# A hybrid decoder block on one core: five operations reordered around the second feed-forward head

## The chip, the cores and the metric

The kernel runs on one core of one Trainium2 chip. The metric is the device time of one execution in microseconds (us), the median of several runs. The profile shows one further execution of the same kernel; its engines are TensorE (PE, with its weight loads as PEld), VectorE (DVE), ScalarE (ACT), GpSimd (POOL) and SyncE (SP, which issues loads).

## The reference

One decoder layer on 512 tokens of width 1024, in float32. A conditioning vector c gives nine vectors: a shift, a scale and a gate for each of three sub-layers.

```python
mod = silu(c) @ w_ada + b_ada                        # nine vectors: sh1 sc1 gt1 sh2 sc2 gt2 sh3 sc3 gt3
u = modulate(rmsnorm(h, g_norm_ffn1), sh1, sc1)
h = h + 0.5 * gt1 * swiglu(u, w_ffn1_in, w_ffn1_out)
u = modulate(rmsnorm(h, g_norm_mix), sh2, sc2)
h = h + gt2 * token_mixing(u, ...)                   # pooling branch and dilated attention, gated, then @ w_out
u = modulate(rmsnorm(h, g_norm_ffn2), sh3, sc3)
h = h + 0.5 * gt3 * swiglu(u, w_ffn2_in, w_ffn2_out)
return rmsnorm(h, g_final)

def rmsnorm(x, g):       return x * rsqrt(mean(x * x, -1) + EPS) * g
def modulate(x, sh, sc): return x * (1 + sc) + sh
def swiglu(u, w_in, w_out):
    a, b = split(u @ w_in, 2)                        # 2816 columns each
    return (silu(a) * b) @ w_out
```

The change lies where token mixing ends and the second swiglu begins: the last output blocks of `merged @ w_out`, the norm of the result, and the first products of `u @ w_ffn2_in`.

## The kernel before, in words

**Layout.** Activations lie feature-major: H[k] is block k (128 features) of the residual stream, with 512 tokens, in two token halves A (0 to 255) and B (256 to 511). A float32 product is made of three matmuls on values split in two: every operand x has a high part (a rounded copy, made by ACT) and a low part (x minus the high part, made by DVE), and `mm3` adds hi·uh, hi·ul and lo·uh. So u, the normed input, exists as UH and UL.

**Weights.** They arrive as chunks of 128x1024 by loads on SP's queue, in a planned order. `split_hi` (ACT, L377, tile whi) and `split_lo` (DVE, L389, tile wlo) turn the next chunk into its two parts in a ring; `split(n)` does both up to chunk n; `look(ahead)` fetches and splits up to `ahead` chunks beyond the current one; `fetch` issues loads into free buffers. Some chunks of the second feed-forward net are sums of others, made by DVE (L312) or by an accumulating copy that POOL issues (L320): its products use a fast matrix multiplication of Strassen's kind, with seven products on 2x2 blocks instead of eight.

**`out_tail`** makes the last output blocks m = 5, 6, 7 of the mixing layer: first half A of each, then half B of each. Per block and half, `tail_step` adds the gated bank to H (DVE, L600) and ACT squares the result (L601); DVE adds the square to the sum of squares (L651, tile AR). The lambdas in `put` are these adds, and `do` runs them. In the middle of the matmuls of block 6, half B, `stats_t` sums half A over partitions by matmuls with ones (L512), takes the root on ACT (L514) and the reciprocal on DVE (L517). Ahead of block 7, half B, `spread` transposes the result over all partitions (L522), and `norm_steps` begins: for each block a norm on DVE (L535), UH on ACT (L547) and UL on DVE (L565).

**`head`** follows: four weight tiles (the first two pairs of columns) times u. Half A goes in twelve steps, the last four of which take blocks 4 to 7 with all four tiles; half B goes in eight steps. The norms of half B are made during half A. After step 8 of half A and steps 2 and 5 of half B a further chunk is split, as far as the ring has room.

**Rows of u.** The first of the block products need u also as a plain float32 array; for half B and for blocks 4 to 7 of half A, ACT writes these rows (L552, tile X). Rows of half B are written at once; those of half A wait in the list `rows`.

**`ffn2`** calls the head, then makes the sums of blocks of u for the fast multiplication: `u_steps` returns four sums (x22, x21, x11, x12) and the pairs of high and low parts (s0 to s3, ACT L757 and DVE L758, tiles SH and SL) made from them. The first seven products (`duo`, with `product`, L794 to L796) take u itself, then the parts of s0 (B), s1 (A), and so on.

**Order.** Every engine runs its instructions in the order in which the program issues them. The order of each queue is written out by hand, and the change edits this order.

Of the kernel before, what the change touches and what calls it, by code (L numbers as in the profile page):

```python
# [11 lines left out]
AF = mybir.ActivationFunctionType  # L12
# [153 lines left out]
class Kernel:  # L166
# [430 lines left out]
    def tail_step(self, m, hs, bank, gate, s):  # L597

        Hm = self.H[m][:, hs]
        self.nc.vector.scalar_tensor_tensor(Hm, bank[:, hs], gate[:, m:m + 1], Hm, op0=OP.mult, op1=OP.add)  # L600
        self.nc.scalar.activation(s, Hm, AF.Square)  # L601

    def out_tail(self, ms, ksrc, gate, nxt, squares, beside=None):


        nc = self.nc
        tiles, starts, put, rest = {}, {}, [], self.spare()
        A, Bh = slice(0, HT), slice(HT, T)
        step = None
        self.held = self.pos  # L610
        for h, hs in enumerate((A, Bh)):
            for m in ms:
                bank = self.nb()
                if h == 0:
                    starts[m] = self.pos
                    tiles[m] = ksrc(m)
                    starts[m + 1] = self.pos
                if h == 0 and m == ms[0]:
                    nc.scalar.preload_act_table(AF.Sqrt)
                behind = h == 1 and m == ms[1]  # L620
                if self.done < self.pos + 4 and not behind:
                    self.split_hi()
                ks = tiles[m]
                if h == 0 and m == ms[0]:
                    self.settle(bank, ks[0][0], ks[0][2])
                for i, (hi, lo, uh, ul) in enumerate(ks):
                    if behind and i == len(ks) // 2:
                        self.stats_t(rest[0], A)
                        if self.done < self.pos + 4:
                            self.split_hi()  # L630
                        if self.half and len(self.half[1]) > 1:
                            self.split_lo(True)
                    if h == 1 and m == ms[2] and i == 0:
                        self.spread(rest[0], A)
                        step = self.norm_steps(nxt, A)
                        if nxt == 2:
                            step.three()
                        step(0)
                        self.split_lo()
                        self.fetch()  # L640
                    self.mm3(bank[:, hs], hi, lo, uh[:, hs], ul[:, hs], i == 0, i == len(ks) - 1)
                if step and m == ms[-1]:
                    step.low()
                    step.high()
                s = squares(m)[:, :HT]
                self.tail_step(m, hs, bank, gate, s)
                if h == 1:
                    self.held = starts[m + 1]
                    if step:
                        step(1 if m != ms[-1] else 3)  # L650
                put.append(lambda s=s, hs=hs: nc.vector.tensor_tensor(self.acc[:, hs], self.acc[:, hs], s, op=OP.add))  # L651
                do = lambda: [put.pop(0)() for _ in range(len(put))]
                if nxt == 2 and h == 0 and m == ms[-1]:
                    do()
                if not behind:
                    self.split_lo()
                    self.fetch()
                if beside and h == 0 and m == ms[0]:
                    beside()
                if h == 0 or m != ms[1]:  # L660
                    do()
        self.stepA = step

    def head(self, n, banks, table, between=(), beside={}):

        nc = self.nc
        A, Bh = slice(0, HT), slice(HT, T)
        self.held = self.pos
        stepA, stepB = self.stepA, self.norm_steps(n, Bh)
        w = [self.take() for _ in banks]  # L670

        both, late = list(range(4)), (0, 1, 2)
        steps = [(k, late) for k in range(4)] + [(k, (3,)) for k in range(4)] + [(k, both) for k in range(4, KT)]
        for h, hs in enumerate((A, Bh)):
            for i, (k, which) in enumerate(steps if h == 0 else [(k, both) for k in range(KT)]):
                if h == 0:
                    if i == 4:
                        self.stats_t(self.spare()[1], Bh)
                        nc.scalar.preload_act_table(table)
                    stepA(min(i, 5) + 2)  # L680
                    if i == 8:
                        self.spread(self.spare()[1], Bh)
                    if i > 7:
                        stepB(i - 8)
                        if n == 2 and i == 8:
                            stepB.low()
                            while self.rows:
                                self.rows.pop(0)()
                else:
                    stepB(k + 3)  # L690
                for f in beside.get((h, i), ()):
                    f()
                for j in which:
                    self.mm3(banks[j][:, hs], *w[j][k], self.UH[k][:, hs], self.UL[k][:, hs], k == 0, k == KT - 1)
                if (h, i) in ((0, 8), (1, 2), (1, 5)):
                    if h and between:
                        between.pop(0)()
                    if n == 2 and (h, i) == (1, 2):
                        stepB.high()
                        stepB.low()  # L700
                    self.split(self.done)
                    self.fetch()
        for f in between:
            f()
        self.held = None
# [68 lines left out]
    def step(self):  # L774

        self.now += 1
        due = [f for t, f in self.put if t <= self.now]
        self.put = [x for x in self.put if x[0] > self.now]
        for f in due:
            f()  # L780
# [421 lines left out]
    def ffn2(self):  # L1202
        self.put, self.now = [], 0
        self.negate(2)
        bk = [self.nb() for _ in range(4)]
        (a11, a12), (a21, a22) = self.U4
        (x22, x21, x11, x12), (s2, s1, s0, s3) = self.u_steps(2)
        self.ready = True
        self.rows.pop(0)()
        self.head(2, bk, AF.Silu, beside={(0, 6): self.whole(a11, 0)})  # L1210
        for f in (x22, s0[0], x21):
            f()
        h0, h1 = (self.ffn_silu(j, bk[2 * j]) for j in range(2))
        for f in (x11, s1[0], s0[1], s1[1]):
            f()
        late = self.block_hidden(0)
        two = lambda: self.look(2)
        b4, b5 = (self.banks[(self.bi + i) % 6] for i in range(2))

        def begin():  # L1220
            two()
            x12()
            s2[0]()
            self.free += self.rawx[1:]

        def posts():
            two()
            self.ffn_post(0, h0, bk[1])
            self.ffn_post(1, h1, bk[3])

        def more():
            self.free += self.rawx[:1]

        def end():
            self.open_first()
            self.banks, self.bi = [bk[1], bk[2], b4, b5, bk[0], bk[3]], 0

        self.ffn(2, 2, ((begin,), (posts, s2[1]), (two, *s3, more), (self.look,), (*late[:4], self.look),
                        (late[4], late[6], self.look, late[5], late[7]), (self.look, end)))

# [1057 lines left out]
```

## Time and profile before

| what | value |
|---|---|
| median of 3 runs | 958.99 us |
| the 3 runs | 957.89, 958.99, 968.86 us |
| the profiled execution, its own time | 969.29 us |
| its span in the profile | 967.5 us |
| mean granted clock of TensorE | 0.999 |
| PE busy | 959.3 us, 99% of the span |
| DVE busy | 842.2 us, 87% |
| ACT busy | 545.4 us, 56% |
| POOL busy | 90.5 us, 9% |

A row of a timeline gives start, length, engine, line, operation, written tile, read tiles, shape and count, and in brackets the idle time of the engine ahead of it with what ended it. A row of the waits gives the waiter, what it waited for, the sum in us, how often, and the longest. A row of the window table gives the window, its length, then busy time and number of instructions for PE, PEld, DVE, ACT and POOL, the granted clock, the share of the DMA engines and their GB/s. Lengths of neighbouring instructions on one engine overlap a little, so the distance between starts tells what an instruction takes of a queue.

### The profile page before, as it was taken

To read this page: it belongs to the slowest core of one execution; us is meant where nothing else is said; L and a number is where in the kernel's file an instruction comes from. 1 tells how busy PE (TensorE), PEld (TensorE's weight loads), DVE (VectorE), ACT (ScalarE), POOL (GpSimd) and SP (SyncE) were. 2 spreads that over 40 slices of the span, in tenths; PEclk is the share of its full clock that TensorE was granted. 3 is DMA by queue.
4 is the path that set the end of the run, shared out by engine and by line. 5 is a ranking of instruction groups with operands and counts; after the bars stand their busy time and mean duration, and the time that the engine had idled before them with its cause. 6 is when DMAs were issued, how large, how long until landed. Compare 5 with 4: busy or idle time off the path is not lost.

```text
span 967.5 us, 18319 instructions
## 1 busy us (share of the span) xinstructions
PE 959.3 (99%) x7352; PEld 907.7 (94%) x7352; DVE 842.2 (87%) x1241; ACT 545.4 (56%) x829; POOL 90.5 (9%) x110
## 2 busy tenths in 40 slices
PE   9999999999999999999999999999999999999997
PEld 7888999999999999788899998999999999999997
DVE  7989999899998788886979768989998988879886
ACT  6453666665745453454565552477755656556555
POOL 0000100100010003007200000011011001000002
PEclk9999999999999999999999999999999999999999
DMA  9856776776868548857365446646766566665632
GB/s 357 283 191 240 209 218 166 207 207 152 223 170 246 174 153 254 260 189 197 77 186 158 137 144 224 206 102 185 200 166 161 140 173 164 166 153 140 163 81 88
DMA packets 55304, 176.81 MB, mean 183 GB/s; under 512 B 7857, under 2 KB 11569, under 8 KB 54962
## 3 DMA queue, kind: packets, MB, share of 16 engines
q1 hardware_dynamic: 44800, 141.82, 44.6%
q0 software_dynamic: 9840, 33.30, 19.2%
q8 instruction: 57, 0.93, 0.4%
q10 hardware_dynamic: 578, 0.53, 0.2%
q14 instruction: 29, 0.24, 0.1%
HBM read 135.36 MB, written 2.24 MB: 142 GB/s over the span
## 4 chain that ended last, share of the span: by engine, by line
PE 90%; DVE 4%; DMA 2%; ACT 1%; issue 1%; POOL 0%; SPq 0%; POOLq 0%; DVEq 0%; ACTq 0%
PE bank L795 15%; PE bank L794 15%; PE bank L796 15%; PE bank L424 6%; PE bank L425 6%; PE bank L426 6%; PE bank L1176 5%; PE bank L1175 5%; PE bank L1177 5%; PE bank L2219 2%; PE bank L2222 2%; PE bank L2224 1%; DVE wlo L389 1%; DMA v<-wada 1%; PE bank L1862 1%
## 5 line engine op out<-in xcount | busy, mean ns | idle before, releaser
L389 DVE TENSOR_TENSOR wlo<-raw,whi 128x1024 fp32r<-128x1024 f32 (+3 forms) x148 | 164.9, 1123 | 37.7 <-ACT whi L377 37.5
L794 PE MATMUL bank<-UH,whi 128*128 128x256 f32 x704 | 195.9, 278 | 0.0
L796 PE MATMUL bank<-UH,wlo 128*128 128x256 f32 x704 | 195.9, 278 | 0.0
L795 PE MATMUL bank<-UL,whi 128*128 128x256 f32 x704 | 195.9, 278 | 0.0
L389 DVE TENSOR_TENSOR wlo<-X,whi 128x1024 fp32r<-128x1024 f32 (+3 forms) x138 | 147.0, 1077 | 25.5 <-ACT whi L377 25.4
L377 ACT ACTIVATE whi<-raw 128x1024 fp32r<-128x1024 f32 (+3 forms) x148 | 141.3, 968 | 22.9 <-DMA raw<-wf1o 6.4
L377 ACT ACTIVATE whi<-X 128x1024 fp32r<-128x1024 f32 (+3 forms) x138 | 127.2, 942 | 42.9 <-DVE X L312 39.1
L794 PEld LDWEIGHTS bank<-UH,whi 128*128 128x128 f32 x704 | 133.5, 190 | 0.2
L795 PEld LDWEIGHTS bank<-UL,whi 128*128 128x128 f32 x704 | 132.2, 188 | 0.0
L796 PEld LDWEIGHTS bank<-UH,wlo 128*128 128x128 f32 x704 | 132.2, 188 | 0.0
L795 PE MATMUL bank<-SL,whi 128*128 128x256 f32 x432 | 120.5, 279 | 0.0
L796 PE MATMUL bank<-SH,wlo 128*128 128x256 f32 x432 | 120.4, 279 | 0.0
L794 PE MATMUL bank<-SH,whi 128*128 128x256 f32 x432 | 120.4, 279 | 0.0
L794 PEld LDWEIGHTS bank<-SH,whi 128*128 128x128 f32 x432 | 82.1, 190 | 0.0
L795 PEld LDWEIGHTS bank<-SL,whi 128*128 128x128 f32 x432 | 81.1, 188 | 0.2 <-DVE SL L758 0.2
L796 PEld LDWEIGHTS bank<-SH,wlo 128*128 128x128 f32 x432 | 81.1, 188 | 0.0
L424 PE MATMUL bank<-UH,whi 128*128 128x256 f32 (+1 forms) x240 | 80.4, 335 | 0.0
L425 PE MATMUL bank<-UL,whi 128*128 128x256 f32 (+1 forms) x240 | 79.2, 330 | 0.1
L426 PE MATMUL bank<-UH,wlo 128*128 128x256 f32 (+1 forms) x240 | 79.1, 330 | 0.0
L802 ACT ACTIVATE ev<-bank 128x512 f32<-128x512 f32 x54 | 32.1, 595 | 54.0 <-PE bank L796 53.8
L1175 PE MATMUL bank<-HI,whi 128*128 128x256 f32 x224 | 62.5, 279 | 0.0
L1176 PE MATMUL bank<-HK,whi 128*128 128x256 f32 x224 | 62.5, 279 | 0.0
(411 smaller groups left out, 2423.7 us busy)
## 6 DMA issues: line engine op xcount, KB each, us to landing
raw<-wmix SPq DMA_DIRECT2D x44, 512.0 KB, 4.2
raw<-wf1i SPq DMA_DIRECT2D x32, 512.0 KB, 5.7
raw<-wf2i SPq DMA_DIRECT2D x29, 512.0 KB, 4.5
ada<-wada SPq DMA_DIRECT2D x24, 512.0 KB, 6.0
X<-raw POOLq DMA_DIRECT2D x24, 512.0 KB, 5.2
xs<-wada SPq DMA_DIRECT2D x17, 512.0 KB, 6.0
X<-wf2i SPq DMA_DIRECT2D x15, 512.0 KB, 4.5
X<-wf1i SPq DMA_DIRECT2D x11, 512.0 KB, 4.3
```

The costliest lines, as they stand in the source:

```text
L377: self.nc.scalar.activation(self.hi[:, y], r[:, x], AF.Copy)
L389: self.nc.vector.tensor_tensor(self.lo[:, y], r[:, x], self.hi[:, y], op=OP.subtract)
L424: M(ps, hi, uh, start=start, stop=False)
L425: M(ps, hi, ul, start=False, stop=False)
L426: M(ps, lo, uh, start=False, stop=stop)
L794: M(o, hi, uh, start=start and p == 0 and k == 0, stop=False, skip_group_check=True)
L795: M(o, hi, ul, start=False, stop=False, skip_group_check=True)
L796: M(o, lo, uh, start=False, stop=k == 3, skip_group_check=True)
L802: copy = lambda o, x, f=1.0: nc.scalar.activation(o, x, AF.Copy, scale=f)
L1175: M(o, hi, uh, start=start and m % 2 == 0 and k == 0, stop=False, skip_group_check=True)
L1176: M(o, hi, ul, start=False, stop=False, skip_group_check=True)
L1177: M(o, lo, uh, start=False, stop=k == 1, skip_group_check=True)
```

## The change

Five edits of order, all in the second head; no instruction is added or removed.

1. *Root ahead of a square.* In `out_tail`, the square of block 5, half B, is held back until `stats_t` has issued the root of half A, and the add of that square runs behind the low part of a chunk, in the middle of block 6.
2. *u's rows behind a split.* In `head`, the deferred rows of u are written after the split and the fetch at step 8 of half A, not ahead of them.
3. At step 2 of half B, the high part of the next chunk is issued, then UL of block 7, then the chunk's low part; before, UL of block 7 came two steps later, behind the low part.
4. *First block sum's low part ahead of the third sum.* In `ffn2`, the low part of s0 is issued ahead of x11.
5. *A chunk ahead of the second.* The call that splits a chunk (`two`) is issued ahead of the high part of s1, not at the start of the first product.

```diff
     def tail_step(self, m, hs, bank, gate, s):
...
-        self.nc.scalar.activation(s, Hm, AF.Square)
+        return lambda: self.nc.scalar.activation(s, Hm, AF.Square)

     def out_tail(self, ms, ksrc, gate, nxt, squares, beside=None):
...
-        tiles, starts, put, rest = {}, {}, [], self.spare()
+        tiles, starts, put, squared, rest = {}, {}, [], [], self.spare()
+        do = lambda: [put.pop(0)() for _ in range(len(put))]
...
                         self.stats_t(rest[0], A)
+                        while squared:
+                            squared.pop(0)()
                         if self.done < self.pos + 4:
                             self.split_hi()
                         if self.half and len(self.half[1]) > 1:
                             self.split_lo(True)
+                        do()
...
-                self.tail_step(m, hs, bank, gate, s)
+                square = self.tail_step(m, hs, bank, gate, s)
+                first = nxt == 2 and h == 1 and m == ms[0]
+                if first:
+                    squared.append(square)
+                else:
+                    square()
...
-                if h == 0 or m != ms[1]:
+                if h == 0 or m != ms[1] and not first:
                     do()

     def head(self, n, banks, table, between=(), beside={}):
...
                         if n == 2 and i == 8:
                             stepB.low()
-                            while self.rows:
-                                self.rows.pop(0)()
...
                     if n == 2 and (h, i) == (1, 2):
                         stepB.high()
                         stepB.low()
-                    self.split(self.done)
+                        self.split_lo()
+                        self.split_hi()
+                        stepB(6)
+                        stepB.low()
+                    self.split(self.done - bool(self.half))
                     self.fetch()
+                    while self.rows:
+                        self.rows.pop(0)()

     def ffn2(self):
...
-        for f in (x11, s1[0], s0[1], s1[1]):
+        two = lambda: self.look(2)
+        for f in (s0[1], x11, two, s1[0], s1[1]):
             f()
         late = self.block_hidden(0)
-        two = lambda: self.look(2)
...
         def begin():
-            two()
             x12()
```

More of the change, by code (lines that the diff above doesn't have):

```diff
@@ L651, in out_tail @@
                 put.append(lambda s=s, hs=hs: nc.vector.tensor_tensor(self.acc[:, hs], self.acc[:, hs], s, op=OP.add))
-                do = lambda: [put.pop(0)() for _ in range(len(put))]
                 if nxt == 2 and h == 0 and m == ms[-1]:
```

## The prediction

> **What bounds the kernel now.** I read the page first, for the engine that carries the end, then one window table, then the waits of TensorE (PE) in the window of the change, then the timelines of PE, VectorE (DVE) and ScalarE (ACT) around each wait.
>
> ```profile
> span 967.5 us, 18319 instructions
> PE 90%; DVE 4%; DMA 2%; ACT 1%; issue 1%; POOL 0%; SPq 0%; POOLq 0%; DVEq 0%; ACTq 0%
> ...
> 612.00:656.00 44.00, 43.74 (x378) 43.13 (x377) 38.66 (x71) 30.28 (x55) 4.02 (x4) 1.00 0.46 122
> 656.00:949.00 293.00, 293.00 (x2493) 293.00 (x2492) 258.96 (x324) 179.51 (x245) 24.35 (x29) 1.00 0.61 154
> ```
>
> PE carries 90% of the chain that ended last. The window from 612 to 656 us holds everything the change touches; there PE is busy 43.74 of 44.00 us, and from 656 to 949 us all of 293.00 (the columns are PE, PEld, DVE, ACT, POOL). So the change can win only what PE waits in this window, and a DVE or ACT that gets ahead there wins nothing afterwards. DVE is busy 38.66 of the 44 us, so it is the engine that makes PE wait.
>
> A busy PE may hide a late start, since a matmul that waits on an operand is partly counted as busy. The waits of the same window give three with PE or its weight loads as the waiter, and the PE timeline gives their true size by the starts:
>
> ```profile
> PEld bank L425 <- DVE UL L565: 0.3, 1, 0.3
> PEld bank L522 <- DVE r L517: 0.3, 1, 0.3
> PEld bank L795 <- DVE SL L758: 0.2, 1, 0.2
> 623.08 0.28 PE L426 MATMUL bank<-v,wlo 128*128 128x256 f32 x1
> 623.48 0.43 PE L522 MATMUL bank<-cst,r 128*128 128x128 f32 x2
> 640.83 0.38 PE L424 MATMUL bank<-UH,whi 128*128 128x256 f32 x1
> 641.35 0.39 PE L425 MATMUL bank<-UL,whi 128*128 128x256 f32 x1
> 641.58 0.28 PE L426 MATMUL bank<-UH,wlo 128*128 128x256 f32 x1
> 652.35 0.28 PE L794 MATMUL bank<-SH,whi 128*128 128x256 f32 x1
> 652.62 0.39 PE L795 MATMUL bank<-SL,whi 128*128 128x256 f32 x1
> ```
>
> 128x256 matmuls normally start 0.115 us apart (18 of them from 626.61 to 628.65 in the next fence, 0.113 each; I use 0.115, since single gaps are 0.11 or 0.12). Against that: the transposes that spread the root (L522) start 0.40 after the matmul ahead of them, 0.29 too late. UL of the second half's third block is 0.52 behind its predecessor, 0.41 too late, and the matmul after it starts 0.23 later, another 0.12: a wait for an operand costs the wait and a restart of 0.12. The low part of the first block sum (SL) is 0.27 behind, 0.16 too late, and I count the same 0.12 behind it. Together 0.29 + 0.53 + 0.28 = **1.10 us**, the most that the change can take off by shortening waits: 0.11% of the span.
>
> **Part 1, the root ahead of a square.** Rows of DVE and ACT, then PE:
>
> ```profile
> 622.47 0.42 ACT L601 ACTIVATE gc<-H 128x256 f32<-128x256 f32 x1 [2.08 <-DVE H L600]
> 622.79 0.24 ACT L514 ACTIVATE r<-bank,eps 128x2 f32<-128x2 f32 x1
> 622.92 0.43 DVE L651 TENSOR_TENSOR AR<-AR,gc 128x256 f32<-128x256 f32 x1 [0.55 <-ACT gc L601]
> 622.93 1.14 ACT L377 ACTIVATE whi<-raw 128x512 fp32r<-128x512 f32 x2
> 623.26 0.16 DVE L517 RECIPROCAL r<-r 128x2 f32<-128x2 f32 x1
> 623.59 0.69 DVE L389 TENSOR_TENSOR wlo<-raw,whi 128x512 fp32r<-128x512 f32 x1 [0.17 <-ACT whi L377]
> 624.19 0.48 DVE L600 SCALAR_TENSOR_TENSOR H<-bank,mod,H 128x256 f32<-128x256 f32 x1
> 625.76 0.48 DVE L565 SCALAR_TENSOR_TENSOR UL<-ev,mod,UH 128x256 fp32r<-128x256 f32 x1
> 627.94 0.48 DVE L565 SCALAR_TENSOR_TENSOR UL<-ev,mod,UH 128x256 fp32r<-128x256 f32 x1
> 621.36 0.60 PE L512 MATMUL bank<-ones,AR 128*128 128x128 f32 x4
> 626.61 0.28 PE L425 MATMUL bank<-UL,whi 128*128 128x256 f32 x1
> 628.65 0.28 PE L425 MATMUL bank<-UL,whi 128*128 128x256 f32 x1
> ```
>
> The sums over partitions (L512) end at 621.36 + 0.60 = 621.96, but the root (L514) stands behind a square (L601) that waits for H until 622.47, and the reciprocal (L517) stands behind the add of that square. With the root first it can start near 622.1 (an estimate: 621.96 and a short way to ACT), end near 622.35, and the reciprocal ends by about 622.6, ahead of the 623.19 at which PE comes to the transposes. The wait of 0.29 goes.
>
> What is late next: the square still starts at 622.47, since H releases it; the copies of the next chunk (whi L377) follow at 622.79 instead of 622.93, 0.14 earlier; DVE's low part (L389) follows at 623.45 instead of 623.59. But the add, which ran from 622.92 in time that DVE had free, now stands behind this low part, in DVE's full stretch. It takes 623.26 - 622.92 = 0.34 of the queue. H of the next block (L600, 624.19) then starts 0.34 - 0.14 = 0.20 later, and so does all that is queued behind: three norms, UL of block 0 (625.76, L565), UL of block 2 (627.94). UL of block 0 would be done at 625.96 + 0.48 = 626.44 and usable about 0.06 later (UL at 640.81 + 0.48 against PE's 641.35, below), at 626.50. PE comes to it at 626.61 - 0.29 = 626.32: a new wait of 0.18 and a restart of 0.12. That is 0.30 given back for 0.29 won. UL of block 2 is usable at 628.14 + 0.54 = 628.68 against 628.65, so a second restart may come on top. **I take 0.0 for this part**; its bounds are -0.29 (DVE is not later, and the gain carries through) and +0.15 (the second restart as well).
>
> The Trainium skill (VectorE: DVE Perf Modes, "The DRAIN you can't avoid") says that the next DVE operation does not start until the pipe of the one before has emptied, and leaves operations that nothing holds to another section. By the plain rule the added step costs the add's whole 0.43 instead of 0.34, and this part would be +0.09 instead of 0.0. The rows 622.92 and 623.26 speak against it: the reciprocal starts 0.34 after the add.
>
> **Part 2, u's rows behind the split.** In step 8 of the head's first half, ACT writes row copies of u ahead of the split of the next chunk:
>
> ```profile
> 635.93 1.69 ACT L552 ACTIVATE X<-ev,mod 128x256 f32<-128x256 f32 x4
> 637.53 1.05 ACT L377 ACTIVATE whi<-raw 128x1024 fp32r<-128x1024 f32 x1
> 636.46 1.22 DVE L312 TENSOR_TENSOR X<-raw,raw 128x1024 f32<-128x1024 f32 x1
> 638.61 1.23 DVE L389 TENSOR_TENSOR wlo<-raw,whi 128x1024 fp32r<-128x1024 f32 x1 [0.94 <-ACT whi L377]
> 640.26 0.51 ACT L547 ACTIVATE UH<-ev,mod 128x256 fp32r<-128x256 f32 x1 [1.68 <-DVE ev L535]
> 640.81 0.48 DVE L565 SCALAR_TENSOR_TENSOR UL<-ev,mod,UH 128x256 fp32r<-128x256 f32 x1 [0.19 <-ACT UH L547]
> ```
>
> Three of the four rows at 635.93 are the deferred ones (blocks 5 to 7 of the first half; the fourth belongs to the block just made). Four take 637.53 - 635.93 = 1.60, so three take 1.20. Behind them the chunk's high part starts at 637.53 and its low part at 638.61, with DVE idle 0.94 for it, and the two norms, UH and UL, on which PE waits at 641.35, come behind that low part. With the rows moved, the high part starts at 636.33 and ends 637.38; the low part then starts when the sum at 636.46 frees DVE, at 637.60, 1.0 earlier. Even with the 0.20 of part 1, UL is usable at 641.35 - 1.0 + 0.2 = 640.55, against a PE that asks at 640.95. **This wait goes whole: -0.53.** The chunk's data are there: DVE adds that raw block to another at 636.46 without a wait. What the moved rows meet: ACT frees at 637.38 + 0.2 + 1.2 = 638.8, and UH of the third block would start at 640.26 - 0.8 = 639.46. Should they collide after all, UH could slip by up to 0.40 before PE notices. The fetch ahead of the moved rows issues one load on SP's queue, after the low part as now, 0.8 earlier; POOL's accumulating copies keep their order. In the first head no row is deferred, no square is held back, and the new call that empties the list of adds finds it empty.
>
> The second edit there, at step 2 of the second half, makes UL of block 7 ahead of a chunk's low part instead of behind it:
>
> ```profile
> 646.16 1.23 DVE L389 TENSOR_TENSOR wlo<-X,whi 128x1024 fp32r<-128x1024 f32 x1 [0.53 <-ACT whi L377]
> ```
>
> The low part (1.14 of the queue) now has UL of block 7 behind it; the UL moves into its 0.53 of idle wait for ACT. PE asks for it five blocks of 12 matmuls, 1.37 each, after 641.35, near 648.2, so it was not late and nothing is won at PE: 0. It shortens DVE's queue by some 0.4. The change of the split's bound by a pending half is no change: with a half pending, both forms finish that half and stop.
>
> **Part 3, the first block sum's low part ahead of the third sum, a chunk ahead of the second.**
>
> ```profile
> 650.21 1.22 DVE L762 SCALAR_TENSOR_TENSOR X<-X 128x1024 f32<-128x1024 f32 x1
> 651.35 2.44 DVE L758 TENSOR_TENSOR SL<-X,SH 128x1024 fp32r<-128x1024 f32 x2
> 653.71 1.22 DVE L389 TENSOR_TENSOR wlo<-X,whi 128x1024 fp32r<-128x1024 f32 x1
> 652.60 0.33 SPq L295 DMA_DIRECT2D X<-wf2i  x1
> ```
>
> DVE makes the third sum (L762, on to 651.35), then the low parts of the first two splits (L758). The first low part moves ahead of the third sum, 1.14 earlier, so it ends before PE asks at 652.46. **The wait goes: -0.28.** The price falls on the second split: its sum is 1.14 later in the order, and the next chunk's copy on ACT and low part on DVE (653.71, 1.14 of the queue) now run ahead of its high and low part. DVE would be through it at 650.21 + 3 x 1.14 + 1.22 = 654.85 with no lead. PE asks for it 24 matmuls of 0.115 after 652.46, at 655.22, and 0.8 earlier if all gains stand: 654.4. DVE's lead by then is 1.0 - 0.2 from part 2 and 0.4 from the second edit, 1.2 in all, so the low part is done at 653.65: slack 0.75. The SP load at 652.60 starts right after the first low part has read its buffer and moves ahead with it.
>
> **The sum.** 0.0 - 0.53 - 0.28 = **-0.8 us**. The profiled execution took 969.29 us, of which 967.5 are the span; it would take 968.5. The runs shown are 957.89, 958.99 and 968.86, so the profiled one lies 10 us above the median, near the third run, with PE at full granted clock (1.00 above). Nothing in the window explains that, and the sum is a difference: on the median it gives 958.99 - 0.8 = **958.2**. The 2% that a measurement of this kernel can tell from no change is 19 us, over twenty times the effect; even the upper bound of the gain, 1.1, is within it.
>
> **Rivals.**
> - *All three waits go* (part 1 carries through because DVE catches up before block 0): -1.1, 957.9. For it: PE had 626.61 against 626.30 as slack, 0.3. Against it: the add is moved from DVE's idle time into its full stretch.
> - *Nothing is won* (the release moves to the next queued operand each time, since DVE has only 5.3 of the 44 us free): between -0.4 and +0.1, 958.8. For it: part 1 does that by my own count. Against: parts 2 and 3 remove DVE idle time (0.94 and 0.53), not only order.
> - *Slower*: the root does not come early enough, and DVE's lag runs through. The point is 622.47: a root that starts later holds the square up, which H alone held before, and then the copies and the low part. If PE's sums reach ACT no sooner than in the row at 622.79, the square starts at 623.03, the copies 0.43 later than now, and with the 0.34 of the add all of DVE's queue is 0.77 late. UL of block 0 is then usable at 627.07 against 626.32: 0.75 + 0.12 - 0.29 = +0.58 in part 1. If ACT's row chain, fed by the same late norms, also eats the lead of part 2, UL at 641.35 is 0.77 late, and with part 3's -0.28 the sum is +0.5, 959.5. Against it: the sums end 0.51 ahead of that point.
>
> **How the numbers follow.** Forecast (-0.5 to -0.95) 0.6, all three 0.15, nothing 0.18, slower 0.07. Every case lies between -1.1 and +0.5, which on the two lower runs is 956.8 to 959.5. But the runs of this one kernel lie 11 us apart, and a median of a few can fall on the upper one, with one in three runs there; 968.86 - 0.8 = 968.1. The likeliest case's own range is 957.0 to 958.5; the range that holds the time 8 times in 10 must reach to the upper run: 956.6 to 968.5. Over 2% faster or slower: none of the cases, 0.01 each for what I don't see; within 2%: 0.98.
>
> **What would show it.** In the profile after: no wait of L522 on L517 near 623; a short new wait of L425 on L565 near 626.3; none near 640.9; the first L552 rows of blocks 5 to 7 behind a whi of 1.05; no wait of L795 on L758 near 651.6, and L758's second low part done a good half microsecond ahead of the third product. Wrong would be: the wait at 640.9 still there (rows were not what held the chunk), or a new one after 654.

## The result and the profile after

| | kernel before | changed kernel |
|---|---|---|
| median | 968.87 us of 22 runs | 958.02 us of 22 runs |
| range | 957.89 to 970.07 | 957.28 to 958.99 |
| runs above 964 us | 12 of 22 | 0 of 22 |
| median of the runs below 964 us | 958.75 (10 runs) | 958.02 |
| the profiled execution, its span | 969.29, 967.5 | 957.47, 955.7 |

The ratio is 0.9935 (95% interval 0.9909 to 0.9961): faster, by less than 2%. The time itself is the one forecast (958.2), but not for the reason given. The runs of the kernel before fall in two groups, near 959 and near 969, with nothing between 960 and 967; the granted clock is 1.00 in both. The changed kernel has only the lower group. Within that group it gains 958.75 - 958.02 = 0.73 us, near the 0.8 of the sum, though the runs of one group spread over 1.5 us, too wide to tell 0.8 from 0.5 or from 1.0; against the median of all runs it gains 10.85.

First the forecast steps. The edits move some lines of the kernel: L794 to L796 of the kernel before are L806 to L808 of the changed one, and L757, L758 and L762 are L769, L770 and L774. In the table of waits of this window no row is left in which PE or its weight loads wait. From the page of the changed kernel, its span and the shares of the chain:

```profile
span 955.7 us, 18320 instructions
PE 97%; issue 1%; ACT 1%; POOL 1%; DVE 0%; POOLq 0%; ACTq 0%
```

The window table of the changed kernel around the change (from and to, then busy us and number of instructions of PE, weight loads, DVE, ACT and POOL, the granted clock, the share of DMA and GB/s):

```profile
612.00:656.00 44.00, 44.00 (x387) 43.89 (x386) 39.80 (x71) 31.91 (x57) 4.21 (x4) 1.00 0.53 134
```

From its PE timeline (start, length, line, operation):

```profile
622.76 0.28 PE L426 MATMUL bank<-v,wlo 128*128 128x256 f32 x1
622.88 0.38 PE L522 MATMUL bank<-cst,r 128*128 128x128 f32 x2
625.86 0.28 PE L424 MATMUL bank<-UH,whi 128*128 128x256 f32 x1
625.98 0.38 PE L425 MATMUL bank<-UL,whi 128*128 128x256 f32 x1
626.20 0.28 PE L426 MATMUL bank<-UH,wlo 128*128 128x256 f32 x1
628.15 0.39 PE L425 MATMUL bank<-UL,whi 128*128 128x256 f32 x1
628.38 0.28 PE L426 MATMUL bank<-UH,wlo 128*128 128x256 f32 x1
651.45 0.28 PE L806 MATMUL bank<-SH,whi 128*128 128x256 f32 x1
651.56 0.28 PE L807 MATMUL bank<-SL,whi 128*128 128x256 f32 x1
```

PE is now 97% of the chain, and busy for all 44.00 us of the window. The transposes (622.88) follow the matmul ahead of them by 0.12: the wait for the root has gone. UL of block 0 (625.98) starts 0.12 after its predecessor, and the matmul behind it 0.22 later; behind UL of block 2 (628.15) the next one starts after 0.23: two restarts of 0.11 to 0.12. SL (651.56) follows at 0.11: no wait. For the steps behind these, first one DVE row of the kernel before, which sets the two clocks against each other, then the DVE timeline of the changed kernel, then that of ACT:

```profile
620.76 1.22 DVE L389 TENSOR_TENSOR wlo<-raw,whi 128x1024 fp32r<-128x1024 f32 x1
```

```profile
620.25 1.22 DVE L389 TENSOR_TENSOR wlo<-raw,whi 128x1024 fp32r<-128x1024 f32 x1
623.88 0.48 DVE L600 SCALAR_TENSOR_TENSOR H<-bank,mod,H 128x256 f32<-128x256 f32 x1
639.46 0.48 DVE L565 SCALAR_TENSOR_TENSOR UL<-ev,mod,UH 128x256 fp32r<-128x256 f32 x1 [0.19 <-ACT UH L547]
648.37 1.23 DVE L770 TENSOR_TENSOR SL<-X,SH 128x1024 fp32r<-128x1024 f32 x1
```

```profile
621.68 0.26 ACT L514 ACTIVATE r<-bank,eps 128x2 f32<-128x2 f32 x1 [1.80 <-PE bank L512]
636.96 1.29 ACT L552 ACTIVATE X<-ev,mod 128x256 f32<-128x256 f32 x3
```

From the same low part H starts 3.43 later before (624.19) and 3.63 after (623.88): 0.20, to the digit of the working. The root runs at 621.68, the three deferred rows of u as a group at 636.96, UL of the third block at 639.46, and the first block sum's low part (648.37) ends 2 us ahead of PE's use of it.

Terms of this size rest on one execution each. DVE's low part at 620.76 starts 0.60 ahead of PE's sums over partitions (L512, 621.36) in the kernel before; in the changed kernel the two are at 620.25 and 621.04, 0.79 apart. No edit acts on either instruction, and over the fourteen profiles of this document that lead of DVE lies between 0.45 and 1.21. In two of the six profiles with the old order of the root, PE does not wait for the root at all.

Now the 10 us. They are in no row of waits. They are in the distance of PE's starts from one matmul to the next (its pace, below), over the whole stretch behind the change. The window table with the number of matmuls, the kernel before and then the changed one:

```profile
652.85:900.00 247.15, 247.15 (x2100) 247.15 (x2100) 223.45 (x271) 152.44 (x201) 22.44 (x26) 1.00 0.65 167
```

```profile
632.60:900.00 267.40, 267.40 (x2362) 267.40 (x2361) 247.25 (x304) 172.15 (x236) 26.67 (x30) 1.00 0.66 165
652.85:900.00 247.15, 247.15 (x2184) 247.15 (x2183) 228.74 (x277) 156.53 (x207) 22.75 (x27) 1.00 0.67 171
```

PE is busy 100% in all three windows. But 2100 matmuls take 247.15 us in the kernel before, 0.1177 each, and 2184 take the same time in the changed one, 0.1132 each. In the kernel before the distance changes at the wait for SL:

```profile
649.52 0.28 PE L794 MATMUL bank<-UH,whi 128*128 128x256 f32 x1
652.13 0.28 PE L796 MATMUL bank<-UH,wlo 128*128 128x256 f32 x1
...
652.85 0.28 PE L796 MATMUL bank<-SH,wlo 128*128 128x256 f32 x1
...
655.44 0.28 PE L794 MATMUL bank<-SH,whi 128*128 128x256 f32 x1
```

The first two rows are the first and the last of 24 matmuls ahead of the wait: 2.61 / 23 = 0.1135. The last two are the ends of 22 distances behind it: 2.59 / 22 = 0.1177.

The slow distance then holds for every product until the tail. 2100 matmuls x 0.0045 = 9.5 us to 900, and in proportion 1.2 more up to the tail near 930: 10.7 of the 11.8 by which the spans differ; 0.8 are the waits, and 0.3 lie ahead of the change (PE's sums start at 621.36 before and 621.04 after). The page shows it only where the means of one matmul are read side by side:

```profile
L794 PE MATMUL bank<-UH,whi 128*128 128x256 f32 x704 | 195.9, 278 | 0.0
```

```profile
L806 PE MATMUL bank<-UH,whi 128*128 128x256 f32 x704 | 194.4, 276 | 0.0
```

Before and after, 278 against 276 ns is all that is left of 4%, since matmuls overlap.

### The profile page after: what moved, and what is told of

Read it like the earlier page. It is cut to its first block, busy times and chain, and to the rows that moved or that the text cites. A ratio compares the mean times of both kernels' runs of the same rounds, so it can differ in the third digit from the quotient of the medians.

```text
span 955.7 us, 18320 instructions
## 1 busy us (share of the span) xinstructions
PE 946.8 (99%) x7352; PEld 896.8 (94%) x7352; DVE 842.3 (88%) x1241; ACT 546.3 (57%) x829; POOL 90.6 (9%) x110
## 4 chain that ended last, share of the span: by engine, by line
PE 97%; issue 1%; ACT 1%; POOL 1%; DVE 0%; POOLq 0%; ACTq 0%
PE bank L806 15%; PE bank L808 15%; PE bank L807 15%; PE bank L424 9%; PE bank L425 9%; PE bank L426 9%; PE bank L1189 5%; PE bank L1187 5%; PE bank L1188 5%; PE bank L2230 2%; PE bank L2233 2%; PE bank L2235 2%; PE bank L1564 1%; PE bank L1615 1%; PE bank L1873 1%; PE bank L1874 1%
## 5 line engine op out<-in xcount | busy, mean ns | idle before, releaser
L806 PE MATMUL bank<-UH,whi 128*128 128x256 f32 x704 | 194.4, 276 | 0.0
L808 PE MATMUL bank<-UH,wlo 128*128 128x256 f32 x704 | 194.4, 276 | 0.0
L806 PEld LDWEIGHTS bank<-UH,whi 128*128 128x128 f32 x704 | 132.2, 188 | 0.2
L808 PEld LDWEIGHTS bank<-UH,wlo 128*128 128x128 f32 x704 | 132.2, 188 | 0.0
L806 PE MATMUL bank<-SH,whi 128*128 128x256 f32 x432 | 119.2, 276 | 0.0
L808 PE MATMUL bank<-SH,wlo 128*128 128x256 f32 x432 | 119.2, 276 | 0.0
L806 PEld LDWEIGHTS bank<-SH,whi 128*128 128x128 f32 x432 | 81.1, 188 | 0.0
L808 PEld LDWEIGHTS bank<-SH,wlo 128*128 128x128 f32 x432 | 81.1, 188 | 0.0
L1189 PE MATMUL bank<-HI,wlo 128*128 128x256 f32 x224 | 61.8, 276 | 0.0
```

Source lines behind the costliest of these rows:

```text
L806: M(o, hi, uh, start=start and p == 0 and k == 0, stop=False, skip_group_check=True)
L808: M(o, lo, uh, start=False, stop=k == 3, skip_group_check=True)
L1189: M(o, lo, uh, start=False, stop=k == 1, skip_group_check=True)
```

## The experiments

Two theories at first. A: a late wait of PE can leave it in the slower pace, which then holds. B: the 10 us belong to the execution (the chip, the memory, the day), and the change only takes off its waits. The lower group is the runs near 959 us, the upper group those near 969. The kernel before ran beside every kernel; over all comparisons 69 of its 134 runs were in the upper group (12 of 22, 19 of 35, 14 of 35, 18 of 29, 6 of 13), some on each of two chips.

Pace and group agree in all fourteen profiles: the five executions of the upper group have 0.118 from some place behind the transposes that spread the root of half B up to the tail, the nine of the lower group have 0.113 (one of them after a short slower stretch, shown below). No run of the kernel before itself was profiled in the lower group.

**The parts one by one.** Edits 4 and 5 alone:

```diff
-        for f in (x11, s1[0], s0[1], s1[1]):
+        two = lambda: self.look(2)
+        for f in (s0[1], x11, two, s1[0], s1[1]):
             f()
         late = self.block_hidden(0)
-        two = lambda: self.look(2)
...
         def begin():
-            two()
             x12()
```

> The kernel before with edits 4 and 5 alone (low part of s0 ahead of x11, the chunk's split ahead of s1). Theory A (pace): the wait of PE for the low part of s0 in the second product can leave PE at a start-to-start distance of 0.118 us instead of 0.113 until the tail, 10 us in all; without that wait every execution lies near 958.7 (0.3 below the lower group of the kernel before), with 0.113 throughout. Theory B (waits only): the 10 us are a matter of the execution and not of this wait; the times still come in two groups, near 958.7 and 968.6.

Measured: 968.55 median, 11 of 12 runs in the upper group; ratio to the kernel before 1.0046 (1.0005 to 1.0086). Neither 958.7 nor half and half. The PE timeline of this kernel:

```profile
653.29 0.28 PE L794 MATMUL bank<-SH,whi 128*128 128x256 f32 x1
655.90 0.28 PE L796 MATMUL bank<-SH,wlo 128*128 128x256 f32 x1
656.01 0.35 PE L794 MATMUL bank<-SH,whi 128*128 128x256 f32 x1
656.20 0.28 PE L795 MATMUL bank<-SL,whi 128*128 128x256 f32 x1
```

Its window table from there:

```profile
656.20:900.00 243.80, 243.80 (x2071) 243.80 (x2071) 220.39 (x269) 150.12 (x198) 21.60 (x25) 1.00 0.65 166
```

The wait for SL has gone, as expected, and with it the change of pace there: the 24 matmuls to 655.90, the second product, took 2.61 / 23 = 0.1135. But a shorter hitch came one product later, in the third, where SL of the second split now stands behind x11 and a chunk's low part: 0.19 from 656.01 to 656.20 instead of 0.11. From there the pace is 243.80 / 2071 = 0.1177. So in this execution the edit only moved the place. Theory A had the wrong wait in mind; whether it has the right kind of cause, the runs below show.

Edit 2 alone, the rows of u behind the split:

```diff
                             stepB.low()
-                            while self.rows:
-                                self.rows.pop(0)()
...
                     self.split(self.done)
                     self.fetch()
+                    while self.rows:
+                        self.rows.pop(0)()
```

> The kernel before with edit 2 alone (the deferred rows of u behind the split). The split and all of DVE behind it come 1.0 us earlier and PE 0.53 earlier, so the wait for the low part of s0 goes too, by 0.4 us of slack. Theory A: every execution near 958.2 (the wait of 0.53 and that of 0.28 gone), pace 0.113 throughout. Theory B: two groups, near 958.2 and 968.1.

Measured: 957.72, 0 of 12 in the upper group, ratio 0.9932 (0.9894 to 0.9969). Its profile has no wait of PE behind the transposes of the head, and 0.1132 from 633 to 900:

```profile
633.00:900.00 267.00, 267.00 (x2358) 267.00 (x2357) 246.87 (x303) 171.53 (x236) 26.65 (x30) 1.00 0.66 165
```

This one moved loop has the whole effect of the change that can be measured. Edit 1 alone, the root ahead of a square (the lines of `tail_step` and `out_tail` in the diff of the change, and no others):

> The kernel before with edit 1 alone (root ahead of a square). DVE is 0.20 us later from the next H on; the wait for the root (0.29) goes and comes back as a wait and restarts at UL of blocks 0 and 2, and the waits at UL of the second half's third block and at the low part of s0 stay. Both theories: two groups, 0.0 to 0.3 us above those of the kernel before (958.5 and 969.2); theory A: the upper group shows 0.118 from the second product on.

Measured: 969.87, 10 of 12 in the upper group, ratio 1.0044 (1.0000 to 1.0089); its two lower runs are at 958.44 and 958.91. In its profile the pace changes at a third place, the wait for UL of the second half's third block:

```profile
638.45 0.28 PE L424 MATMUL bank<-UH,whi 128*128 128x256 f32 x1
641.06 0.28 PE L426 MATMUL bank<-UH,wlo 128*128 128x256 f32 x1
641.66 0.39 PE L425 MATMUL bank<-UL,whi 128*128 128x256 f32 x1
```

The window table behind it:

```profile
641.90:900.00 258.10, 258.10 (x2193) 258.10 (x2193) 233.68 (x286) 160.55 (x215) 22.44 (x26) 1.00 0.64 163
```

24 matmuls to 641.06 at 2.61 / 23 = 0.1135, then 258.10 / 2193 = 0.1177. In the kernel before the same wait (641.35) left the pace at 0.113; so a wait may or may not change it.

**The wait put back.** The changed kernel with another order:

```diff
-        for f in (s0[1], x11, two, s1[0], s1[1]):
+        for f in (x11, two, s0[1], s1[0], s1[1]):
```

> The changed kernel, with the low part of s0 issued behind x11 and behind the chunk's low part, so that PE waits for it again, for about 0.4 us, in the second product. Theory A: part or all of the executions go to the slower pace from the second product on, near 968.5, the rest near 958.5. Theory B: 958.5 to 958.6 in all, the wait and its restart, and the pace stays 0.113.

Measured: 960.07, 5 of 12 in the upper group (969.41 to 970.81), the others around 959.02. The wait was longer than expected; in the PE timeline it is the idle time in the bracket:

```profile
652.82 0.38 PE L807 MATMUL bank<-SL,whi 128*128 128x256 f32 x1 [0.97 <-DVE SL L770]
```

That restores the upper group in a kernel that had none, though this execution (958.86) is of the lower one: its pace stays 0.113 behind the wait. With weights late in place of u's parts, as follows, PE waits in the third product for a weight load:

```diff
-        for f in (s0[1], x11, two, s1[0], s1[1]):
+        for f in (s0[1], x11, self.fetch, self.split_hi, s1[0], s1[1]):
...
             s2[0]()
+            self.split_lo()
```

> The changed kernel with the low part of the third product's chunk behind s1's low part and behind x12, so that in the third product PE waits about 0.85 us for a weight load (the low weights), with u's parts there in time. Theory A, if any wait of PE can shift the pace: part of the executions near 969.5, the rest near 959. If only a wait for the moving operand does: all near 959.

In its PE timeline:

```profile
655.42 0.39 PE L808 MATMUL bank<-SH,wlo 128*128 128x256 f32 x1 [0.78 <-DVE wlo L389]
```

Measured: 959.39, 2 of 12 in the upper group (969.47 and 970.59). The wait (0.78 idle) is one for weights, so a wait for weights seems able to do it too. That rests on two runs; the profiled one (958.63) is of the lower group and keeps 0.113.

**An extra matmul as a remedy.** In the kernel before, ahead of the fourth product, one matmul of 240 columns into a spare bank, in a form that the kernel has elsewhere (L430):

```diff
+            if beside and i == 3:
+                self.settle(self.spare()[0], w[0][0], self.UH[0])
```

> The kernel before with one more matmul of 240 columns into a spare bank, ahead of the fourth product, behind both late waits; the waits stay. Theory A (each wait of PE behind the last transposes can leave PE at 0.118 instead of 0.113, and the pace holds until the next irregular matmul): the pace may be 0.118 for at most 6 us and then goes back; every execution within 957.5 to 959.5. Theory B (the slow pace is a matter of the execution): half of the executions near 969. If one irregular matmul only draws the pace anew, half of them stay near 969 as well, but with the pace changing at that matmul in some profiles.

Measured: 969.10, 8 of 12 in the upper group: no remedy. The profile of one of the eight:

```profile
655.28 0.28 PE L794 MATMUL bank<-SH,whi 128*128 128x256 f32 x1
657.88 0.28 PE L796 MATMUL bank<-SH,wlo 128*128 128x256 f32 x1
```

The window table behind the extra matmul:

```profile
658.10:900.00 241.90, 241.90 (x2056) 241.90 (x2055) 218.26 (x267) 147.07 (x195) 21.61 (x25) 1.00 0.65 167
```

In this execution the pace had survived both waits: 24 matmuls to 657.88 in 2.60, 0.113. The extra matmul itself changed it, to 241.90 / 2056 = 0.1177. The same place with 256 columns, the length of all others:

```diff
+            if beside and i == 3:
+                self.nc.tensor.matmul(self.spare()[0][:, :HT], w[0][0], self.UH[0][:, :HT], start=True, stop=True, skip_group_check=True)
```

> The same place, the same extra matmul with 256 columns instead of 240, like all others around it. Theory A, if what resets the pace is the odd length: no effect, half of the executions or more near 969, 0.1 above the kernel before. If any extra matmul resets it: all within 957.5 to 959.5.

Measured: 959.37, 3 of 12 in the upper group, where the kernel before had 14 of 35 beside it: no clear effect. Its profiled execution (958.38) has both late waits and keeps 0.113 behind them. To part the extra matmul from the waits, each of the two was put into the changed kernel, which has no wait there, with the same added lines. The odd one:

> The changed kernel, in which PE waits for nothing from the second half of the head on, with one extra matmul of 240 columns ahead of the fourth product. If an odd length shifts PE from one pace to the other (as the one profile of the same matmul in the kernel before shows, 0.113 ahead of it and 0.118 behind it): all 12 executions near 969, 0.118 from that matmul on. If it draws the pace anew: about half. If only waits set the pace: none, 958.1.

Its PE timeline:

```profile
654.20 0.28 PE L806 MATMUL bank<-SH,whi 128*128 128x256 f32 x1
656.81 0.28 PE L808 MATMUL bank<-SH,wlo 128*128 128x256 f32 x1
```

The window table behind the odd matmul:

```profile
658.00:900.00 242.00, 242.00 (x2057) 242.00 (x2056) 217.84 (x265) 146.11 (x193) 21.59 (x25) 1.00 0.65 166
```

Measured: 968.62 (967.94 to 969.84), all 12 in the upper group. 24 matmuls to 656.81 at 0.1135, then the odd one, then 242.00 / 2057 = 0.1176. The even one:

> The same with 256 columns. By all theories no execution near 969: 958.1, 0.113 throughout. If any extra matmul can shift the pace, some near 969.

Measured: 957.96 (957.39 to 959.38), 0 of 12. So at this place one matmul of 240 columns in place of 256 cost 10 us in all 12 runs, with no wait in it. (It also reads other columns, 16 to 255 where the even one reads 0 to 255; the runs don't part the two.) The rule is not general: the kernel has nine more such matmuls (L430) ahead of the change, from 101.86 to 608.91, and in every profile the pace behind each of them is 0.1135 to 0.1146, never 0.118; at 367.51 of the kernel before it is 0.113 ahead of it too. This is theory B's end: the pace is set inside the kernel, and no run of 58 without a late wait or an odd matmul behind the head's transposes (the changed kernel, edit 2 alone, the even matmul, and the early add below) was in the upper group, against 69 of 134 of the kernel before.

**A remedy that works.** All profiles have 0.113 behind the transposes that spread the root of half B (0.1133 or 0.1134 a matmul over the next 6 us in each of the fourteen, the ten taken ahead of the added matmuls in the changed kernel among them). Ahead of them it is 0.117 to 0.118 in each, over the ten distances between PE's sums of half B (L512) and the transposes (L522). In the changed kernel, the first two rows lie ahead of the transposes and the last two behind them:

```profile
630.77 0.28 PE L425 MATMUL bank<-UL,whi 128*128 128x256 f32 x1
631.95 0.28 PE L426 MATMUL bank<-UH,wlo 128*128 128x256 f32 x1
...
632.52 0.28 PE L426 MATMUL bank<-UH,wlo 128*128 128x256 f32 x1
634.56 0.28 PE L426 MATMUL bank<-UH,wlo 128*128 128x256 f32 x1
```

That is 1.18 / 10 = 0.118, then 2.04 / 18 = 0.113. Three profiles (edit 1 alone, the late weights, the even matmul) are at 0.118 from a restart at UL of block 0 or 2 on, 2 to 4 us ahead of PE's sums, and at 0.113 behind the transposes: the late operands of part 1 cost little, since the transposes follow soon. So two such transposes were put at the same place of the kernel before:

```diff
+            if beside and i == 3:
+                for t in (0, P):
+                    nc.tensor.transpose(self.spare()[0][:, t:t + P], self.r4[:, :1].to_broadcast([P, P]), self.ident)
```

> The kernel before, both late waits in place, with two more transposes of 128 columns (the form of the spread of the root) into a spare bank ahead of the fourth product. In all ten profiles so far the pace behind the spread's transposes in the head was 0.113. If they set the pace whatever it was: all executions between 958 and 960, with 0.118 at most from a wait to them. If they only shift it from one to the other: half near 969 as before.

Measured: 958.83 (957.99 to 959.46), 0 of 12, ratio 0.9927 (0.9893 to 0.9961), with both late waits in place. The profiled execution had 0.113 ahead of the added transposes as well as behind them, so they do not merely switch from one pace to the other. And the odd matmul and the transposes behind each other, in the changed kernel (the same added lines, with i == 3 for the first and i == 6 for the second):

> The changed kernel with the odd matmul of 240 columns ahead of the fourth product and two transposes of 128 columns ahead of the seventh. If the odd matmul sets 0.118 and the transposes set 0.113 whatever was ahead of them: 0.118 for three products of 24 matmuls between the two, 0.113 behind, all executions near 958.7 (0.3 us for the slow stretch, 0.4 for the extra matmuls and their restart above 958.0). If the transposes do not set it, all stay near 968.6.

The PE timeline between the two additions:

```profile
657.39 0.28 PE L806 MATMUL bank<-UH,whi 128*128 128x256 f32 x1
665.75 0.28 PE L808 MATMUL bank<-UH,wlo 128*128 128x256 f32 x1
```

The window table behind the transposes:

```profile
666.00:900.00 234.00, 234.00 (x2067) 234.00 (x2066) 214.89 (x261) 146.13 (x194) 22.45 (x26) 1.00 0.67 170
```

Measured: 958.48 (958.04 to 959.56), 0 of 10. Between the two, 72 matmuls took 8.36 / 71 = 0.1177 each; behind the transposes it is 234.00 / 2067 = 0.1132. One execution shows the pace set both ways.

**The add in DVE's idle time.** The changed kernel with the add ahead of the chunk's parts:

```diff
                             squared.pop(0)()
+                        do()
                         if self.done < self.pos + 4:
...
                             self.split_lo(True)
-                        do()
```

> The changed kernel with the add of the held square ahead of the chunk's low part, in DVE's idle time between the reciprocal and that low part. By the working of part 1, DVE's H of the next block then starts 0.34 earlier than in the changed kernel, the wait and the restarts at UL of blocks 0 and 2 go, and PE gains 0.23: near 957.8, pace 0.113 to the end in every execution. Rival: the add waits for the square (until 622.9) and holds the low part up, and nothing is won: 958.0.

The DVE timeline of this kernel:

```profile
620.85 1.22 DVE L389 TENSOR_TENSOR wlo<-raw,whi 128x1024 fp32r<-128x1024 f32 x1
624.14 0.48 DVE L600 SCALAR_TENSOR_TENSOR H<-bank,mod,H 128x256 f32<-128x256 f32 x1
```

Its PE timeline:

```profile
626.24 0.39 PE L425 MATMUL bank<-UL,whi 128*128 128x256 f32 x1
626.46 0.28 PE L426 MATMUL bank<-UH,wlo 128*128 128x256 f32 x1
```

Measured: 957.84 against 958.02: not to be told apart. From the same low part H starts 3.29 later, 0.34 less than in the changed kernel, as worked out. But UL of block 0 still costs a restart (0.22 from 626.24 to 626.46), and PE gained nothing that can be measured. The profile does not settle whether the idea is at fault: in this execution DVE's low part (620.85) leads PE's sums (621.30) by 0.45, against 0.79 in the changed kernel's, which is the same 0.34 lost before the edit acts. No version beats the changed kernel clearly: this one, edit 2 alone and the changed kernel lie within 0.3 us.

## Why the prediction was right, and where it was not

- *The three waits.* Part 1 came out in its parts: the wait for the root gone, H 0.20 later, most of it given back at UL of blocks 0 and 2. But the new wait of 0.18 at block 0 did not show (0.12 from start to start); the price was two restarts and 0.03 at block 2, about 0.26 where the working had 0.30. DVE's lead in that execution was 0.19 greater, which is as much as the missing wait. Part 2 came out: UL of the third block is ready without a wait, and DVE's low part behind the copy has no idle time ahead of it. Part 3 came out in the changed kernel, where DVE has the lead (the second split's low part is done at 653.10, over 1 us ahead of PE's use of it at 654.28). Measured -0.73 in the lower group, -0.8 forecast.
- *The slack of part 3.* The text gave the second split's low part as the price, 0.75 of slack with the lead of part 2. The run with edits 4 and 5 alone shows the case without that lead: the hitch came there, in the third product. The working had it as harmless even without lead (usable at 654.91, PE at 655.22). It came 656.20 - 642.29 = 13.91 behind PE's wait for the third block's UL (642.29 in that kernel), where the working had 654.91 - 641.35 = 13.56: 0.35 too early.
- *The step that failed* is the last of the sum: "Nothing in the window explains that, and the sum is a difference." The window did hold the explanation. The working read single gaps as "0.11 or 0.12" and took 0.115 for all. Single gaps, printed to 0.01 us, look alike at both paces; a count tells them apart, and the quoted row from 656 to 949 us has one: 293.00 / 2493 = 0.1175, against the 0.113 that the text counted at 627. The pace is 0.113 ahead of the wait for SL and 0.118 behind it, and the quoted row at 652.62 is the place where one turns into the other. With 2,400 matmuls behind it, that is a term of -10.7 us for those executions, and it was left out.
- *The bound of 1.10 us* fails for the same reason. "All of 293.00 us busy" was taken to mean that nothing can be won behind 656; it says only that PE was never without a matmul in flight.
- *The rivals.* All three waits gone, nothing won and slower did not occur. None of them had the pace in it. The time lies in the likeliest case's own range because the changed kernel has only the lower group, which the text had no reason to expect. It was luck, too, that two of the three runs it started from were of the lower group: the sum was taken from their median of 958.99, where the median of 22 runs is 968.87.

The Trainium skill (Perfetto Trace Analysis, "Identifying the Most-Contended Engine") warns that matmul busy time is no good measure of how close a kernel is to its roofline, and names two others instead: the matmul work done, as a share of what the window could hold at peak, and the busy share of weight loads. The warning holds here. The first of the two is, in a stream of equal matmuls, the count per microsecond that shows the loss. The second does not show it: in the windows from 652.85 to 900 weight loads are busy 247.15 of 247.15 us in both kernels, at 4% different speed.

The Trainium skill (TensorE: Matmul & The Clock Gate, "Back-to-back issue gap") gives N / 2.4 + 2.5 ns for the isolated gap of a warm PE, an estimate of 109 ns for 256 columns; it says that in a stream of weight loads and matmuls both set the spacing, and has no figure for 256 columns there. These runs show two for the same instruction at the same granted clock, 113 and 118 ns.

## What to carry to other kernels

Judge a busy PE by matmuls per microsecond, window by window, and not by its busy share: a step in that figure marks the place of a lasting loss. As here, a short late operand can cost far more than its wait where a long regular stream of matmuls follows: take the wait away, or put something behind it that runs of that kernel show to restore the pace (here two 128-column transposes). Take a term of a few tenths of a microsecond from more than one profile, since the lead of one engine over another differs by as much from execution to execution. And where runs of one kernel fall in two groups, profile one of each before calling it noise.

## What the runs showed of the hardware

- PE runs one stream (a 128x128 weight load and a 256-column matmul by turns) at two paces, 0.1133 and 0.1178 us a matmul, at a granted clock of 0.998 to 1.000. Either holds for over 2000 matmuls (from 632 us on in the changed kernel, from 653 us on in the kernel before).
- In kernels with late waits of 0.1 to 1.1 us, part of the executions went from the faster to the slower (from 2 of 12 to 11 of 12, by kernel); three profiles show the change at the wait itself, behind the transposes of half B. A 240-column matmul at one place did it in 12 of 12, a 256-column one there in none of 12, while nine other 240-column matmuls have 0.1135 to 0.1146 behind them. Behind the two 128-column transposes that spread the root of half B the pace is 0.113 in every profile, with 0.117 to 0.118 ahead of them; none of the 22 runs with two more such transposes behind the last wait or odd matmul was in the upper group.
- Not settled: what in PE or in its reads differs between the paces, why the same wait changes the pace in one execution and not in another, why the 240-column matmul changes it at one place and not at the nine others, and whether an odd matmul turns the slower pace into the faster one, as the 4 lower runs of 12 with that matmul in the kernel before would allow.
